# A hybrid decoder step: token sums on one engine, a denser threshold search, and value projections tied to the gathered scores

## Chip, core and metric

The kernel runs on one core of a Trainium2 chip. A core has TensorE (PE, matrix products into PSUM), VectorE (DVE), ScalarE (ACT), GpSimd (POOL) and SyncE (SP, which issues transfers); they share the on-chip memory SBUF and work from queues of their own, in order. The metric is the device time of one execution in microseconds; lower is better.

## The reference, cut to what matters

The step handles 1024 prompt tokens and 8 x 4 new tokens (`T = 1024`, `NS = 32`, together `TT = 1056` columns) of width 1024. After a conditioned norm, `h`, everything starts from one projection:

```python
u = h @ w_in       # split into qa, ka, va, za, qi, ki, wi, qr, kr, vr, zr, ga, gr
y_a = sparse_attention(qa, ka, va, top-256 keys by index_scores(qi, wi, ki)) * silu(za)
y_r = group_norm(retention(rotary(qr), rotary(kr), vr)) * g_ret * silu(zr)
merged = sigmoid(ga) * (y_a @ w_pa) + sigmoid(gr) * (y_r @ w_pr)
x = x + gate * (merged @ w_out);  y = rms_norm(x, g_final)
```

The prompt attends to its own keys; each new token also attends to 1024 cached keys and values that are gathered page by page. Retention runs over 8 heads, two at a time. Outputs are the tokens, the new key and value rows and the retention states, all in fp32.

## The kernel before

All large products are made in three terms from split operands: `wh`/`wl` for weights, `HH`/`HL` for tokens (a rounded high part and the rest), lines 216 to 220. A plain block of 128 output columns ("a projection") is made by `project_parts` in three chunks of 352 tokens, 24 matmuls each. Its weights are loaded as `ws`, rounded by ScalarE (L204), and the rest is taken by VectorE or GpSimd (L205); `order` lists which block's weights come next.

Instructions are traced in program order and then put into each engine's queue by a planner that works with estimated times and prefers what was traced first. `tc.issue_after(x)` keeps the instructions that it encloses behind x on x's engine. Pools of tiles have a fixed number of buffers (`bufs`); a tile whose place belonged to another waits until that one is read for the last time.

The stages, in order of time on the profiled execution:

1. Norm, index keys and queries, index scores `SC` of the prompt's blocks and `SCS` of the new tokens (to about 140 us).
2. *Sums of tokens* (`sums_of_tokens`, `last_sums`, L747 to L776). `paired_gates` makes pairs of 128-column blocks by a scheme with seven half-size products in place of eight. It needs sums and differences of the token blocks: `whole_of` joins a high and a low part (GpSimd), VectorE adds and subtracts (L756, L758, L760, L772, L774), ScalarE rounds (L740, L775), VectorE or GpSimd takes the rest (L741, L776). Meanwhile TensorE makes gate blocks 2 and 3, which ScalarE passes through tanh (L729).
3. *Paired blocks* (`paired_gates`): gate blocks 4 to 11 in four pairs, product tiles `sl`, weight forms on GpSimd (L797 to L816). Results are added by VectorE, passed through tanh and written to memory (`TG`).
4. *Retention* (`retention`, `pair`): for each of four head pairs the blocks KR, QR, VR, ZR, the chunked recurrence, and the norm, whose last instruction is `normed[p]` (L686). The attention's query block QA and key block KA of the same index fill TensorE's waits (`split_rows`, `key_rows`). Rotations use one buffer `rot` of 1056 KB; `key_rows` uses half of the same buffer for the key tile x.
5. *Search for the 256th largest score* (`pick_all`): 31 steps, one bit each. In a step VectorE counts five blocks (L1035), ScalarE counts two by signs (L1041), and small VectorE instructions set the next threshold. The steps are tied to `marks`, one for each finished chunk or product of stages 2 to 4. Behind the last step the sample rows are marked (`exact(1)`, `finish(6)`); `mark_rest` marks the prompt's six blocks (`exact(0)`, `finish(5)` to `finish(0)`, L1063 to L1089) into the masks `BI`.
6. *Gathered keys* (`past_scores`): for eight groups of four sequences' half pages, GpSimd gathers cached keys (L1221), TensorE turns them (L1252), ScalarE and VectorE copy them (L1254), TensorE scores them (L1230). The value blocks VA are projected after `past_scores(1)` in program order (L1307 to L1310); their tiles lie in the memory of the scores.
7. Gathered values, gates 12 to 15 and ZA (to about 870 us), the prompt's attention with the output of retention, and the output product.

`token_rows` turns a block into token rows for the outputs: TensorE transposes, ScalarE copies into a tile `tk` (L695), SyncE writes it out (L697).

## Time and profile before

| | |
|---|---|
| median of 3 runs | 1167.2 us (1165.26 to 1172.75) |
| profiled execution | 1164.71 us, span of the instructions 1162.9 us |
| mean granted TensorE clock | 0.981 |
| busy share of the span | PE 94%, PEld 85%, DVE 62%, ACT 42%, POOL 30% |
| the chain that ended last | PE 72%, DVE 13%, DMA 8%, ACT 3%, issue 3% |
| read / written in device memory | 141.49 / 43.33 MB |

Times in the profile are microseconds from the start of the span. A wait row reads "who waited <- what ended the wait: total, times, longest". A row of a group reads "line engine operation out<-in shapes xcount | busy us, mean ns | idle before us <-releaser". A timeline row is "start, duration, engine, line, operation", with the idle time ahead of it in brackets and what ended it. PEld is TensorE's loading of weights, which lies beside the products.

### The profile page before, as it was taken

To read this page: it belongs to the slowest core of one execution; us is meant where nothing else is said; L and a number is where in the kernel's file an instruction comes from. 1 tells how busy PE (TensorE), PEld (TensorE's weight loads), DVE (VectorE), ACT (ScalarE), POOL (GpSimd) and SP (SyncE) were. 2 spreads that over 40 slices of the span, in tenths; PEclk is the share of its full clock that TensorE was granted. 3 is DMA by queue.
4 is the path that set the end of the run, shared out by engine and by line. 5 is a ranking of instruction groups with operands and counts; after the bars stand their busy time and mean duration, and the time that the engine had idled before them with its cause. 6 is when DMAs were issued, how large, how long until landed. Compare 5 with 4: busy or idle time off the path is not lost.

```text
span 1162.9 us, 20931 instructions
## 1 busy us (share of the span) xinstructions
PE 1091.4 (94%) x8234; PEld 987.2 (85%) x8234; DVE 724.6 (62%) x1683; ACT 487.3 (42%) x945; POOL 352.2 (30%) x272
## 2 busy tenths in 40 slices
PE   6989988999999999999897898999999999999997
PEld 5767787999999999999797885777998888799776
DVE  6766399998467464865997124310327777587675
ACT  6565444664444444444231242211315666443111
POOL 0021378755524534222211234243103333200000
PEclk9989998999999999999998899999999999999999
DMA  9946212437237247247132889487666540258331
GB/s 310 292 111 177 74 49 72 132 129 219 55 125 222 56 140 204 58 133 218 50 112 83 261 250 313 146 300 272 227 242 215 217 173 21 90 179 286 121 143 55
DMA packets 159480, 189.98 MB, mean 163 GB/s; under 512 B 19013, under 2 KB 127245, under 8 KB 158294
## 3 DMA queue, kind: packets, MB, share of 16 engines
q1 hardware_dynamic: 149232, 152.35, 42.0%
q0 software_dynamic: 9856, 35.66, 9.0%
q8 instruction: 65, 1.06, 0.4%
q10 hardware_dynamic: 294, 0.63, 0.1%
q14 instruction: 33, 0.27, 0.1%
HBM read 141.49 MB, written 43.33 MB: 159 GB/s over the span
## 4 chain that ended last, share of the span: by engine, by line
PE 72%; DVE 13%; DMA 8%; ACT 3%; issue 3%; POOL 1%; SPq 0%; DVEq 0%; ACTq 0%; POOLq 0%
PE pj L218 10%; PE pj L220 10%; PE pj L219 10%; PE sl L838 6%; PE po L1411 3%; PE pj L1187 3%; PE pj L1188 3%; PE pj L1189 3%; PE pj L1570 3%; PE pj L1571 3%; PE pj L1572 3%; PE tr L1394 2%; DMA out<-tk 2%; PE str L1252 2%; DMA kv<-in_cache_v,idx 2%
## 5 line engine op out<-in xcount | busy, mean ns | idle before, releaser
L218 PE MATMUL pj<-hh,wh 128*128 128x352 f32 (+1 forms) x976 | 322.8, 331 | 12.8 <-ACT rot L481 6.6
L220 PE MATMUL pj<-hh,wl 128*128 128x352 f32 (+1 forms) x976 | 320.2, 328 | 0.0
L219 PE MATMUL pj<-hl,wh 128*128 128x352 f32 (+1 forms) x976 | 318.6, 326 | 0.0
L218 PEld LDWEIGHTS pj<-hh,wh 128*128 128x128 f32 x976 | 186.0, 191 | 22.8 <-issue 8.1
L220 PEld LDWEIGHTS pj<-hh,wl 128*128 128x128 f32 x976 | 186.1, 191 | 5.3 <-issue 4.2
L219 PEld LDWEIGHTS pj<-hl,wh 128*128 128x128 f32 x976 | 186.2, 191 | 1.1 <-issue 0.8
L1035 DVE TENSOR_SCALAR_CACHE_REDUCE bi<-sc,cand 128x896 bf16<-128x896 f32 (+4 forms) x155 | 135.6, 875 | 2.8
L205 POOL TENSOR_TENSOR wl<-ws,wh 128x1024 fp32r<-128x1024 f32 x31 | 76.4, 2463 | 198.6 <-ACT wh L204 193.7
L204 ACT CAST wh<-ws 128x1024 fp32r<-128x1024 f32 (+1 forms) x57 | 52.7, 928 | 86.4 <-PE pj L219 50.4
L1381 POOL TENSOR_SCALAR lg<-lg,st 128x1024 f32<-128x1024 f32 (+7 forms) x64 | 47.8, 755 | 120.1 <-DVE st L1380 107.8
L205 DVE TENSOR_TENSOR wl<-ws,wh 128x512 fp32r<-128x512 f32 (+1 forms) x26 | 25.6, 987 | 57.9 <-ACT wh L204 57.7
L1379 ACT ACTIVATE lg<-lg,st 128x1024 f32<-128x1024 f32 (+7 forms) x64 | 49.5, 774 | 25.0 <-DVE st L1378 23.3
L1570 PE MATMUL pj<-woh,MH 128*128 128x512 f32 (+1 forms) x136 | 51.4, 378 | 0.0
L1571 PE MATMUL pj<-wol,MH 128*128 128x512 f32 (+1 forms) x136 | 51.2, 377 | 0.0
L1572 PE MATMUL pj<-woh,ML 128*128 128x512 f32 (+1 forms) x136 | 51.2, 376 | 0.0
L1221 POOL DMA_INDIRECT kv<-in_cache_k,idx x32 | 30.7, 960 | 54.5 <-PE str L1252 47.3
L1221 POOL DMA_INDIRECT kv<-in_cache_v,idx x32 | 30.1, 941 | 55.0 <-PE sx L1282 43.9
L1394 PE MATMUL tr<-C,lg 128*128 128x128 f32 x288 | 43.6, 276 | 1.6 <-POOL lg L1381 0.5
L1041 ACT ACTIVATE bi<-sc,cand 128x1024 bf16<-128x1024 f32 x31 | 35.6, 1149 | 18.2 <-DVE cand L1116 18.1
L1254 DVE COPY kt<-str 128x512 f32<-128x512 f32 x32 | 22.1, 691 | 32.7 <-PE str L1252 25.1
L1252 PE MATMUL str<-C,kv 128*128 128x128 f32 x256 | 35.3, 279 | 6.8 <-DVE kt L1254 6.8
L1394 PEld LDWEIGHTS tr<-C,lg 128*128 128x128 f32 x288 | 33.3, 140 | 9.5 <-issue 2.4
(395 smaller groups left out, 2366.5 us busy)
## 6 DMA issues: line engine op xcount, KB each, us to landing
ws<-in_w_in SPq DMA_DIRECT2D x51, 512.0 KB
rot<-in_rot SPq DMA_DIRECT2D x8, 1056.0 KB
x<-in_w_ada SPq DMA_DIRECT2D x16, 512.0 KB
wst<-in_w_out SPq DMA_DIRECT2D x12, 512.0 KB
TG<-raw SPq DMA_DIRECT2D x16, 264.0 KB
u<-TG SPq DMA_DIRECT2D x8, 528.0 KB
t<-TG SPq DMA_DIRECT2D x8, 528.0 KB
x<-in_x_prompt SPq DMA_DIRECT2D x8, 512.0 KB
```

Source lines behind the costliest of these rows:

```text
L205: (nc.vector if k == 4 or not third[0] and len(order) % 3 else nc.gpsimd).tensor_sub(wl[:, :, :n], ws[:, :, :n], f32(wh[:, :, :n]))
L218: nc.tensor.matmul(p, wh[:, k], HH[k][:, sl], start=(k == 0), stop=False)
L219: nc.tensor.matmul(p, wh[:, k], HL[k][:, sl], start=False, stop=False)
L220: nc.tensor.matmul(p, wl[:, k], HH[k][:, sl], start=False, stop=(k == KT - 1))
L838: nc.tensor.matmul(x[:, 512 * g:512 * g + HB // 2], wk, mv[:, c:c + HB // 2], start=(k == 0 and term == 0), stop=(k == 3 and term == 2))
L1035: nc.vector.tensor_scalar(junk[:n, :W], sc, thr[:n, j:j + 1], 0.0, op0=op, op1=OP.add, accum_out=cnt[:n, j:j + 1])
L1221: nc.gpsimd.indirect_dma_start(out=t.rearrange("p s c -> p (s c)"), out_offset=None, in_=cache.rearrange("g (r s) h d -> (g r) (s h d)", s ...
L1252: nc.tensor.transpose(x[:, n * i + 128 * s_:n * i + 128 * s_ + 128], kst[:, s_, 128 * (p + i):128 * (p + i) + 128], ident)
L1394: nc.tensor.transpose(x[:, 128 * (j - j0):128 * (j - j0) + 128], lg[:, j % 2, 128 * (j // 2):128 * (j // 2) + 128], ident)
L1570: nc.tensor.matmul(x, MH[:, k, tk], wh[:, k], start=(k == 0), stop=False)
L1571: nc.tensor.matmul(x, MH[:, k, tk], wl[:, k], start=False, stop=False)
L1572: nc.tensor.matmul(x, ML[:, k, tk], wh[:, k], start=False, stop=(k == KT - 1))
```

## The change

- **Sums of tokens**: `whole_of` and the two GpSimd instructions of `last_sums` go to VectorE.
- **Paired blocks**: the fourth pair is no longer gates 10 and 11 but query blocks QA 0 and 1. Their results are split (ScalarE copy, VectorE sub) and written to the query rows instead of going through tanh. Gates 10 and 11 are made whole later: gate 10 behind the last head pair, gate 11 behind the value blocks.
- **Search**: marks start behind gates 2 and 3, there are 97 of them, and the steps are tied to every third mark eight times and then to every two and a half. `mark_rest` is tied behind the last pair's norm.
- **Key blocks**: `key_rows` is a generator with tiles of its own (`raw`); the low part goes chunk by chunk through the tile `zt` to memory. In head pairs 0 and 1 it fills TensorE's waits instead of QA. For the last block the token rows are copied to separate places of the rotation's buffer (`room`) instead of the one-buffer tile `tk`.
- **Value blocks**: blocks 1, 2 and 3 and gate 11 are tied behind the second, fourth, sixth and seventh score product of the gathered keys.

```diff
-    paired = [(j, j + 1) for j in range(4, 12, 2)]
+    paired = [(O_GA + 128 * j, O_GA + 128 * j + 128) for j in range(4, 10, 2)] + [(O_QA, O_QA + 128)]
     after_pairs = []
     for p in range(4):
-        after_pairs += [o + 128 * p for o in (O_KR, O_QR, O_VR, O_ZR, O_QA, O_KA)]
-    after_pairs += [O_VA + 128 * p for p in range(4)]
+        after_pairs += [o + 128 * p for o in (O_KR, O_QR, O_VR, O_ZR) + (O_QA, O_KA)[p < 2:]]
+    after_pairs += [O_GA + 1280] + [O_VA + 128 * p for p in range(4)] + [O_GA + 1408]
...
             for p in range(4):
-                rows = split_rows(gp, O_QA + 128 * p, p, q_rows, qs)
+                keys = key_rows(gp, rp, p, 1)
+                rows = split_rows(gp, O_QA + 128 * p, p, q_rows, qs) if p > 1 else keys
                 pair(rp, RC, O, SD, p, rows)
-                for _ in rows:
-                    pass
-                key_rows(gp, rp, p, rp.tile([128, 2 * TT], F32, name="rot", bufs=1)[:, :TT], 1)
+                for r in (rows, keys):
+                    for _ in r:
+                        pass
+            gates(gp, (10,))
...
-    def token_rows(tl, x, p, out_p, out_s, dst, bufs=2):
+    def token_rows(tl, x, p, out_p, out_s, dst, bufs=2, room=None):
...
-            tk = tl.tile([128, 4, 128], F32, name="tk", bufs=bufs)
+            if room is None:
+                tk = tl.tile([128, 4, 128], F32, name="tk", bufs=bufs)
+            else:
+                tk = room[:, 128 * t0:128 * t0 + 512].rearrange("p (t c) -> p t c", c=128)
...
-    def key_rows(pool, tl, p, x, bufs=2):
-        for _ in split_rows(pool, O_KA + 128 * p, p, k_rows, ks, x):
-            pass
-        token_rows(tl, x, p, k_out, ks_out, None, bufs)
+    def key_rows(pool, tl, p, bufs=2):
+        h, x = [pool.tile([128, TT], d, name="raw", bufs=rows_kept[0]) for d in (F32R, F32)]
+        rows = slice(128 * p, 128 * p + 128)
+
+        def use(c, y):
+            sl = slice(c * CH, c * CH + CH)
+            m = min(sl.stop, T) - sl.start
+            low = tl.tile([128, CH], F32, name="zt", bufs=2).bitcast(F32R)
+            nc.scalar.copy(h[:, sl], y)
+            nc.vector.tensor_sub(low, y, f32(h[:, sl]))
+            nc.scalar.copy(x[:, sl], y)
+            nc.sync.dma_start(KD[rows, 1, sl.start:sl.start + m], f32(low[:, :m]))
+            if c == 2:
+                nc.scalar.copy(ks[:, p], y[:, CH - NS:])
+        yield from project_parts(O_KA + 128 * p, use)
+        nc.sync.dma_start(KD[rows, 0], f32(h[:, :T]))
+        room = tl.tile([128, 2 * TT], F32, name="rot", bufs=1) if p == 3 else None
+        token_rows(tl, x, p, k_out, ks_out, None, bufs, room)
...
     def whole_of(x, t):
-        nc.gpsimd.tensor_tensor(t, f32(x[0]), f32(x[1]), op=OP.add)
+        nc.vector.tensor_tensor(t, f32(x[0]), f32(x[1]), op=OP.add)
...
-            nc.gpsimd.tensor_tensor(b, f32(x_), f32(y_), op=OP.subtract)
+            nc.vector.tensor_tensor(b, f32(x_), f32(y_), op=OP.subtract)
             nc.vector.tensor_tensor(a, a, b, op=OP.add)
             nc.scalar.copy(h, a)
-            nc.gpsimd.tensor_sub(l, a, f32(h))
+            nc.vector.tensor_sub(l, a, f32(h))
...
-                nc.scalar.activation(t, t, AF.Tanh, scale=0.5)
-                j = paired[n][r]
-                nc.sync.dma_start(TG[128 * j:128 * j + 128, HB * c:HB * c + HB], t)
+                f0 = paired[n][r]
+                if f0 >= O_GA:
+                    nc.scalar.activation(t, t, AF.Tanh, scale=0.5)
+                    nc.sync.dma_start(TG[f0 - O_GA:f0 - O_GA + 128, HB * c:HB * c + HB], t)
+                else:
+                    h = temp().bitcast(F32R)
+                    m_ = HB if c == 0 else T - HB
+                    nc.scalar.copy(h, t)
+                    nc.vector.tensor_sub(t.bitcast(F32R), t, f32(h))
+                    if c == 1:
+                        nc.vector.tensor_tensor(qs[:, f0 // 128], f32(h[:, m_:]), t[:, m_:], op=OP.add)
+                    for places, x in zip(q_rows, (f32(h), t)):
+                        for d in places:
+                            nc.sync.dma_start(d[f0:f0 + 128, HB * c:HB * c + m_], x[:, :m_])
...
-                after = marks[3 * i + 4 if i < 10 else 34 + 3 * (i - 10)]
+                after = marks[3 * i + 2 if i < 8 else 28 + (5 * (i - 8)) // 2]
...
         def mark_rest():
-            exact(0)
-            for j in range(NP - 2, -1, -1):
-                finish(j)
+            with tc.issue_after(normed[3].ins):
+                exact(0)
+                for j in range(NP - 2, -1, -1):
+                    finish(j)
...
-        marks = []
         with ExitStack() as s2:
...
             ps = ps1.enter_context(tc.tile_pool(name="pss", bufs=1, reuse_waits="tile", space=PSUM))
+            marks = []
             paired_gates(gp, stp, moved, lambda: ps.tile([128, 1024], F32, name="sl", bufs=4))
...
-    for p in range(4):
+    def value_rows(p):
         x = tl.tile([128, TT], F32, name="raw", bufs=rows_kept[0])
         project(O_VA + 128 * p, lambda c, y: nc.scalar.copy(x[:, c * CH:c * CH + CH], y))
         token_rows(tl, x, p, v_out, vs_out, VD)
+
+    value_rows(0)
+    for p, n in ((1, 1), (2, 3), (3, 5)):
+        with tc.issue_after(scored_[n].ins):
+            value_rows(p)
+    with tc.issue_after(scored_[6].ins):
+        gates(tl, (11,))
```

`scored_` collects the last matmul of each call of `scores` in `past_scores`.

More of the change, by code (lines that the diff above doesn't have):

```diff
@@ L459, in _hybrid_step @@
     q_rows = [[d[:, o] for o in (0, 1)] for d in QD]
-    k_rows = [[KD[:, o]] for o in (0, 1)]
     ZD = dram.tile([512, TT], F32, name="ZD")
@@ L470, in _hybrid_step, with split_rows @@
     rows_kept = [2]
-    def split_rows(pool, f0, p, dst, new, x=None):
+    def split_rows(pool, f0, p, dst, new):
         hl = [pool.tile([128, TT], F32R, name="raw", bufs=rows_kept[0]) for _ in "hl"]
@@ L479, in use @@
             nc.vector.tensor_sub(hl[1][:, sl], y, f32(hl[0][:, sl]))
-            if x is not None:
-                nc.scalar.copy(x[:, sl], y)
             if c == 2:
@@ L786, in load @@
                 t = (pool if n % 2 else wp).tile([128, KT, 128], F32, name="ws", bufs=2)
-                nc.sync.dma_start(t, wcols(w_in, KT, O_GA + 128 * paired[n][i], 128))
+                nc.sync.dma_start(t, wcols(w_in, KT, paired[n][i], 128))
                 w += [t[:, :4], t[:, 4:]]
@@ L841, in paired_gates @@
             y = inner(x)
+            temp = lambda: pool.tile([128, HB], F32, name="u", bufs=4)
             def kept(u, base):
@@ L849, in result @@
                 nc.vector.tensor_tensor(halves_(t), halves_(base), y, op=OP.add)
-                nc.scalar.activation(t, t, AF.Tanh, scale=0.5)
-                j = paired[n][r]
-                nc.sync.dma_start(TG[128 * j:128 * j + 128, HB * c:HB * c + HB], t)
-            temp = lambda: pool.tile([128, HB], F32, name="u", bufs=4)
+                f0 = paired[n][r]
[12 more added lines that the diff above has]
+                            nc.sync.dma_start(d[f0:f0 + 128, HB * c:HB * c + m_], x[:, :m_])
             if m == 1:
@@ L1147, in _hybrid_step @@
         retention(gp)
-        assert len(marks) == 106, len(marks)
+        assert len(marks) == 97, len(marks)
         drain()
@@ L1238, in scores @@
         return last
+    scored_ = []
     def past_scores(G):
@@ L1255, in past_scores @@
                 KK.append(kt)
-            scores(G, lambda b4, p: KK[b4][:, p], n, slice(n * u, n * u + n),
+            last = scores(G, lambda b4, p: KK[b4][:, p], n, slice(n * u, n * u + n),
                    BM[G][:, :PAST].rearrange("p (q s) -> p s q", s=8)[:, QU * u:QU * u + QU],
-                   st[G][:, u - 1:u] if u else BIGNEG, st[G][:, u:u + 1])
+                          st[G][:, u - 1:u] if u else BIGNEG, st[G][:, u:u + 1])
+            scored_.append(last)
     valued = []
```

## The prediction

> **What bounds the kernel now.** On the page TensorE's row of tenths stands at nine nearly everywhere, so time can come only from the slices that are lower. Behind the start-up these lie in two groups, and I cut the span there at the stages (stretch, its length, busy time of PE, PEld, DVE, ACT and POOL with counts, granted clock, DMA share, GB/s):
>
> ```profile
> 143.00:200.00 57.00, 47.03 (x299) 46.32 (x298) 56.35 (x68) 23.63 (x43) 49.24 (x32) 0.88 0.20 61
> ...
> 262.00:548.00 286.00, 285.90 (x2157) 273.48 (x2156) 176.70 (x412) 130.56 (x240) 110.28 (x53) 1.00 0.48 141
> 548.00:597.00 49.00, 44.01 (x384) 40.93 (x382) 44.88 (x85) 15.68 (x31) 8.00 (x5) 0.93 0.26 66
> 597.00:660.00 63.00, 51.52 (x300) 49.95 (x299) 37.86 (x70) 13.22 (x26) 16.89 (x11) 0.90 0.52 168
> ...
> 692.00:740.00 48.00, 38.63 (x435) 27.03 (x428) 20.82 (x39) 13.72 (x24) 23.68 (x26) 1.00 0.90 302
> ```
>
> In the sums (143 to 200) VectorE is full and TensorE idles 10.0 us; in 262 to 548 TensorE is the bound; in the last retention pair (548 to 660) it idles 5.0 and 11.5 us; over the gathered keys (692 to 740) 9.4 us. The list of waits says who ended these:
>
> ```profile
> PE str L1252 <- DVE kt L1254: 6.8, 18, 0.4
> PE pj L218 <- ACT rot L481: 6.6, 1, 6.6
> PE sl L838 <- ACT u L857: 5.6, 1, 5.6
> PE pb L601 <- DVE tmp L607: 5.0, 1, 5.0
> ...
> PE pj L218 <- ACT raw L1309: 4.1, 1, 4.1
> ...
> PE pj L218 <- ACT raw L729: 2.1, 1, 2.1
> ```
>
> ScalarE ends most of them, but it is itself held; its timeline names by whom:
>
> ```profile
> 616.14 0.45 ACT L481 COPY rot<-pj 128x352 f32<-128x352 f32 x1 [7.79 <-DVE raw L479]
> ...
> 654.47 0.25 ACT L695 COPY tk<-pt 32x128 f32<-32x128 f32 x1 [8.12 <-DMA out<-tk]
> ```
>
> So at 611 the cause is VectorE's marking, and at 652 the one-buffer tile tk, whose write to memory must land before the next copy (L1309 stands behind it on ScalarE's queue). Each long wait costs twice, for the clock falls behind it:
>
> ```profile
> 156.00:164.00 8.00, 5.92 (x28) 5.89 (x28) 7.89 (x6) 3.66 (x7) 7.41 (x5) 0.79 0.16 68
> ```
>
> This stretch holds the 2.1 us wait alone; 0.21 of 8 us is 1.7 us lost. Summed so, the clock takes 57 x 0.12 = 6.8 us in the sums and 49 x 0.07 + 63 x 0.10 = 9.7 us in the last pair. Part of it falls on idle time; I take 5.7 and 8.2, the latter as 2.9, 2.7 and 2.6 behind the three waits of that pair. The Trainium skill (TensorE: Matmul & The Clock Gate, "What's actually happening") has the rate halve after an idle window of about 3.4 us: by it a 2.1 us wait would cost no clock, and the sums would have 1.7 us less to give. The stretch above disagrees, and the sum goes by the stretch.
>
> **The change part by part.** Removable in all: sums 10.0 + 5.7 = 15.7 us, last pair 16.5 + 8.2 = 24.7 us, gathered keys 9.4 us.
>
> *Sums on VectorE.*
>
> ```profile
> 142.95 0.14 DVE L1054 TENSOR_SCALAR base<-cnt 32x1 int32<-32x1 f32 x1 [5.10 <-ACT bis L1041]
> ...
> 146.85 0.70 DVE L741 TENSOR_TENSOR tl<-u,th 128x528 fp32r<-128x528 f32 x1
> ...
> 148.83 1.83 DVE L756 TENSOR_TENSOR u<-u 128x528 f32<-128x528 f32 x1
> ...
> 167.46 0.40 PE L838 MATMUL sl<-hh,wh 128*128 128x264 f32 x2
> ...
> 188.98 72.72 PE sl L838 x576
> ...
> L744 POOL TENSOR_TENSOR u<-hh,hl 128x528 f32<-128x528 f32 x8 | 12.2, 1540 | 0.7 <-DVE tl L741 0.7
> L773 POOL TENSOR_TENSOR u<-hl,tl 128x528 f32<-128x528 f32 x4 | 6.6, 1660 | 2.0 <-DVE tl L741 2.0
> L744 POOL TENSOR_TENSOR ws<-hh,hl 128x528 f32<-128x528 f32 x4 | 6.0, 1491 | 2.7 <-DVE u L758 2.7
> L776 POOL TENSOR_TENSOR hl<-u,hh 128x528 fp32r<-128x528 f32 x4 | 5.8, 1439 | 0.0
> ```
>
> A VectorE sum of 128x528 takes 0.70 us alone and 1.83 us beside a GpSimd sum. Twenty GpSimd instructions (30.6 us) become twenty of VectorE: 14 us. With the 32 that it has, 52 x 0.70 = 36.4 us; about eight weight forms that stay on GpSimd may hold it some 1.1 us each, 9 us. VectorE waits idle until 142.95 and can begin near 138, so it ends at about 183; the first 36 instructions end near 168. The first products start at 167.46 after a 2.1 us wait and its 1.7 us of clock, so at 163.7 without them. Three need no sum (24 matmuls and 72.72 x 24 / 576 = 3.0 us each), which gives 172.7; the fourth finds its sums, the sixth (178.7) may wait for the last ones. The first search step also leaves this stage, since marks begin behind it. I keep 3 us: **-12.7**. Bounds: -15.7, and 0 if the forms hold every sum.
>
> *Query pair, gate 10 and 11 exchanged.* The four pairs keep their products; two query blocks take the place of gates 10 and 11, which are made whole later: TensorE's work is the same. Their four results swap a tanh for one copy and one VectorE sub each, 4 x 0.70 us, against six subs saved later; sixteen DMAs leave instead of four, in place of eight later. Between 262 and 548 nothing of it ends a wait: 0. Pairs 0 and 1 have two chunks of filler less, which the next pair's projections replace.
>
> *Denser search.*
>
> ```profile
> L1035 DVE TENSOR_SCALAR_CACHE_REDUCE bi<-sc,cand 128x896 bf16<-128x896 f32 (+4 forms) x155 | 135.6, 875 | 2.8
> ...
> 624.89 0.45 ACT L1309 COPY raw<-pj 128x352 f32<-128x352 f32 x1 [3.36 <-PE pj L220]
> 628.71 0.45 ACT L1309 COPY raw<-pj 128x352 f32<-128x352 f32 x1 [3.36 <-PE pj L220]
> ```
>
> 155 counts are 31 steps of five: 4.4 us of counts, with their small instructions about 5.3 us. A chunk of a projection takes 3.8 us, so a step per 2.5 chunks is one per 9.6 us instead of 11.5. 262 to 548 gets two steps more in 23 us less: (176.7 + 10.6) / 263 = 71% of VectorE, under TensorE's cover. The last step falls on the second chunk of the last pair's values, one chunk later in that pair than now, so the marking of the sample rows, which follows at once, still meets the products behind L607. I halve that wait (5.0 + 2.9 of clock): **-4.0**, bounds -7.9 and 0.
>
> *Marking behind the last norm; tk in the rotation's tile.* At L481 VectorE has nothing to mark any more: **-9.3** (6.6 + 2.7). With a place of its own for each group, ScalarE's copies of the last key tile no longer wait for memory: **-6.7** (4.1 + 2.6). Key tiles in raw free the rotation's buffer for the next pair's load; no TensorE wait stands there: 0.
>
> What is late next? The marking itself (groups of VectorE between 578 and 632; then the norm's place in the first and the last pair, idx, the first gather and the gathers' median landing):
>
> ```profile
> L1086 DVE TENSOR_TENSOR_SCAN ra<-eq 128x1024 f32<-128x1024 bf16 (+5 forms) x6 | 9.7, 1623 | 0.1
> L1088 DVE SCALAR_TENSOR_TENSOR ra<-sc,base,ra 128x1024 f32<-128x1024 f32 (+5 forms) x6 | 7.4, 1237 | 0.0
> L1087 DVE SCALAR_TENSOR_TENSOR ra<-ra,rem,eq 128x1024 f32<-128x1024 f32 (+5 forms) x6 | 7.4, 1230 | 0.1
> L1035 DVE TENSOR_SCALAR_CACHE_REDUCE eq<-sc,base 128x1024 bf16<-128x1024 f32 (+5 forms) x7 | 6.9, 987 | 0.0
> L1085 DVE TENSOR_SCALAR eq<-sc,base 128x1024 bf16<-128x1024 f32 (+5 forms) x6 | 3.4, 574 | 0.0
> L1089 DVE TENSOR_SCALAR bi<-ra 128x1024 bf16<-128x1024 f32 (+5 forms) x6 | 3.1, 518 | 0.0
> ...
> 626.29 0.39 DVE L1211 TENSOR_SCALAR idx<-gidx 128x8 int32<-128x8 int32 x4 [0.98 <-DMA kd<-raw]
> ...
> L655 PE MATMUL pt<-vm,kd x16: 587/613/638, 328.1 to 596.6; 32*64 32x512 f32 x16
> ...
> L683 PE MATMUL pt<-C,O x36: 243/272/327, 345.2 to 638.6; 128*128 128x128 f32 x32, 32*128 32x32 f32 x4
> ...
> 639.58 1.04 POOL L1221 DMA_INDIRECT kv<-in_cache_k,idx  x1 [3.26 <-issue]
> ...
> kv<-in_cache_k,idx POOLq DMA_INDIRECT x32, 6.4
> ```
>
> The six groups sum to 38 us. In the first pair the norm's transposes (L683) begin 17 us behind L655; in the last one, in the marking's company, they end 42 us behind it. So without company the last norm ends near 618 instead of 639, and the marking, which now waits for it, runs from there to 656 or later. The value tiles lie where the scores were: the first over the three smallest blocks, which are marked after the largest, so it is free after some two thirds, near 643; the last only at the end. Until then TensorE has from 597 on 6.75 chunks of queries, keys and gate 10 (26 us), two value chunks into its two banks (7.6 us) and 2.5 us of transposes: to 633. The first gather needs idx (it waited for a key tile's write, KD from raw, above), whose place gate 10's raw tile may now hold until its own write lands near 628; 6.4 us later it is there. So TensorE stands still for 2 to 10 us; I take 5 and 2.5 of clock: **+7.5**. Behind the marking on VectorE's queue come the copies of the gathered keys (L1254), for which the transposes wait: at worst a scan of 1.6 us for each of the first eight gathers, 13 us, at best nothing; I take **+5**.
>
> *Values held.* Three value blocks and gate 11 now stand between the scores instead of ahead of them, and fill TensorE's short waits for L1254. The holds bind TensorE's queue alone. The weight splits of these blocks move along, onto GpSimd's queue among the gathers or VectorE's behind the marking; seven buffers of gathers cover them, without which one such split delays a gather by its length. SyncE gets eight more issues for the keys' low parts and the value writes later; nothing on the path waits for it there, but the value rows of the new tokens must land before the second phase, beside gate 11 as cover. The first two of eight steps stay bare, so I take two thirds of 9.4: **-6.3**; bounds -9.4 and 0.
>
> Sum: -12.7 - 4.0 - 9.3 - 6.7 + 7.5 + 5 - 6.3 = -26.5. The profiled execution took 1164.71 us (span 1162.9), 2.5 us under the median of 1167.2; between 1138.2 and 1140.7 I say **1139 us**.
>
> **The rivals.** *All waits go and none comes*: 15.7 + 24.7 + 9.4 = 49.8 us off, 1117. For it: none of the fills is short on paper; against: the 38 us of marking have to stand somewhere.
>
> *The marking takes the place of what it held before.* If the first value tile too waits for all of it (23 us from 633 to 656) and the copies pay their 13 us, then 36 us stand against the 34.1 that the last pair and the gathered keys have to give (24.7 + 9.4): the sums alone remain, 1167.2 - 12.7 = 1154.5. For it: the memory that both share; against: fillers and gathers are there before 643.
>
> *Gathers starved.*
>
> ```profile
> 670.64 1.57 POOL L1221 DMA_INDIRECT kv<-in_cache_k,idx  x1 [3.12 <-PE str L1252]
> ```
>
> One gather's issue took 1.57 us, beside a VectorE sub, against 0.94 otherwise. With the marking beside the gathers, the steps L1085 and L1089 (6.5 us) could hold the first ones up: 1139 + 6.5 = 1145. The Trainium skill (SBUF — State Buffer, "Who interferes with whom") says so of such instructions: the port pair is an exclusive lock, and GpSimd writes its descriptors through it.
>
> *Slower: the keys' low parts.* They now go through tile zt, two buffers, each to land in memory before its next use.
>
> ```profile
> 443.58 4.97 DMA out<-tk
> ...
> 646.02 8.35 DMA out<-tk
> ```
>
> Two chunks cover 7.6 us. A landing of 5.0 us is hidden; 8.4 costs 0.8 a chunk. From about 11 us on, twelve chunks would stall 3.4 us each, VectorE's queue with the search behind them: +41, 1180. For it: the freed rotation buffer lets 1056 KB loads run at the same time. Against: both rows are shorter, and the longer one stood among gathers.
>
> *It doesn't do it*: each engine's order is fixed beforehand from estimated times; if it comes out with the same blockages, 1165.
>
> **How the numbers follow.** Forecast 0.50 (1127 to 1150), all gone 0.12, marking in the way 0.18, starved 0.07, same blockages 0.06, slower 0.07. The range 1117 to 1160 leaves out the slower case, the unchanged one and a tail below. 1% (11.7 us) is about what a measurement here tells from no change; the marking case straddles that line, two thirds on the faster side: faster 0.81, same 0.12, slower 0.07.
>
> **What would show it.** Right: no TensorE wait over 3 us between 143 and 200, granted clock above 0.95 there, L741 and L756 near 0.7 us; no wait on L481 or for tk; L1086 to L1089 after the last L686; projections between the L1252 groups. Wrong: a wait for the value tiles' copies or for gathers above 10 us; waits for zt; VectorE full in 262 to 548 with TensorE idle.

## The result, and the profile after

The changed kernel took 1150.8 us in the median of four runs (1147.99 to 1153.95), the kernel before 1166.58 us beside it: a ratio of 0.9858, 95% interval 0.982 to 0.9896. It is faster, by 15.8 us where 28 were forecast. The profiled execution took 1151.78 us (span 1150.0, against 1162.9). The spans differ by 12.9 us only, and four variants below that add next to nothing (experiments 2, 3, 7 and 8) have ratios of 0.989 to 0.991, so some 13 us is the better estimate of what the change is worth.

I cut both spans at the same four events: the end of the index scores, the end of the paired products (end of A), the end of the last head pair's state products (end of B, the retention) and the end of the gathered keys' scores (end of C). Columns as in the prediction: stretch, length, busy time of PE, PEld, DVE, ACT and POOL with counts, granted clock, DMA share, GB/s. First the windows of the kernel before, then of the changed one:

```profile
140.40:261.69 121.29, 111.32 (x817) 110.61 (x818) 116.73 (x206) 66.44 (x116) 90.39 (x63) 0.94 0.29 92
261.69:597.18 335.49, 330.40 (x2542) 314.79 (x2540) 222.05 (x498) 146.24 (x270) 118.35 (x58) 0.99 0.45 130
597.18:739.28 142.10, 121.02 (x969) 105.54 (x969) 65.08 (x117) 39.55 (x75) 49.87 (x44) 0.95 0.71 229
```

```profile
141.76:256.49 114.73, 106.92 (x817) 106.71 (x818) 104.41 (x198) 60.86 (x107) 79.13 (x45) 0.97 0.31 100
256.49:572.12 315.63, 305.02 (x2389) 291.53 (x2387) 228.09 (x496) 144.02 (x269) 113.83 (x56) 0.98 0.45 130
572.12:727.49 155.37, 142.88 (x1122) 127.28 (x1122) 78.49 (x144) 45.04 (x84) 53.45 (x45) 0.97 0.68 219
```

B lost 153 products and C gained 153; at 3.8 us for a chunk of 24 these are 24.2 us of work that only moved. Without them A changed by -6.6, B by +4.3 (315.63 + 24.2 - 335.49) and C by -10.9 us (155.37 - 24.2 - 142.10). What comes before and behind adds +1.4 and -1.1; together -12.9, the difference of the spans. The sums, then, gave half of what was forecast, and the retention got no shorter. How much longer it got is less sure than +4.3: variants below with the same code there scatter from 309.7 to 317.2 us in B, against 311.3 (335.49 - 24.2) in the one trace of before.

The list of waits of the changed kernel, the largest behind the start-up (who waited <- what ended it: total, times, longest):

```profile
PE pb L600 <- DVE tmp L606: 9.6, 4, 3.8
PE sl L854 <- POOL wh L832: 7.8, 1, 7.8
PE str L1283 <- DMA kv<-in_cache_k,idx: 5.1, 2, 3.2
PE str L1283 <- ACT kt L1285: 4.6, 8, 0.7
```

L600 (L601 before) waited once before (5.0 us, last pair) and now waits in all four pairs. Gone are the waits for the rotation's copy (6.6) and behind the tile tk (4.1), and of the key transposes' wait for copies (6.8 on VectorE) 5.1 is left. New are a weight form of GpSimd and the gathers. The timelines of GpSimd and VectorE name what stood behind these two (start, duration, engine, line):

```profile
153.99 19.10 POOL L832 TENSOR_TENSOR wh<-ws,wh 128x512 fp32r<-128x512 f32 x1 [6.79 <-ACT wh L831]
173.05 1.27 POOL L832 TENSOR_TENSOR wl<-ws,wl 128x512 fp32r<-128x512 f32 x1
...
307.43 2.33 POOL L205 TENSOR_TENSOR wl<-ws,wh 128x1024 fp32r<-128x1024 f32 x1
...
608.23 1.19 POOL L1250 DMA_INDIRECT kv<-in_cache_k,idx  x1 [16.76 <-DVE idx L1240]
```

```profile
154.56 0.70 DVE L757 TENSOR_TENSOR tl<-u,th 128x528 fp32r<-128x528 f32 x1
...
171.27 0.70 DVE L790 TENSOR_TENSOR u<-u 128x528 f32<-128x528 f32 x1
...
306.40 0.61 DVE L1063 TENSOR_SCALAR_CACHE_REDUCE bi<-sc,cand 128x384 bf16<-128x384 f32 x1
...
306.94 3.21 DVE L576 SCALAR_TENSOR_TENSOR zsT<-zt,zsT 128x352 f32<-128x352 f32 x1
...
382.91 3.42 DVE L576 SCALAR_TENSOR_TENSOR zsT<-zt,zsT 128x352 f32<-128x352 f32 x1
...
457.12 0.51 DVE L576 SCALAR_TENSOR_TENSOR zsT<-zt,zsT 128x352 f32<-128x352 f32 x1
...
462.04 1.95 DVE L576 SCALAR_TENSOR_TENSOR zsT<-zt,zsT 128x352 f32<-128x352 f32 x1
...
592.67 0.25 DVE L685 SCALAR_TENSOR_TENSOR tmp<-pt,gT,zsT 128x32 f32<-128x32 f32 x1 [2.29 <-PE pt L682]
592.84 0.14 DVE L1091 TENSOR_SCALAR low<-base 128x1 f32<-128x1 f32 x1
...
607.20 0.38 DVE L1240 TENSOR_SCALAR idx<-gidx 128x8 int32<-128x8 int32 x4
```

VectorE's sums now follow one another at 0.70 us without a pause, 28 of them from 154.56 to 171.97, and one GpSimd sub that takes 1.27 us behind them takes 19.1 beside them. The marking begins right behind the last norm, as the tie says, but the gather indices (L1240) stand 14 us into it on VectorE's queue, so the first gather starts at 608. VectorE's mask products (L606) free the PSUM tiles for which L600 waits. The zsT instruction (the pair's gate) right ahead of them takes 3.2, 3.4 and 1.95 us in pairs 0 to 2, where the shortest (an earlier chunk of pair 2) takes 0.51, and the last of a search step's five counts (L1063) stands right ahead of it. Pair 0 before the change, with ScalarE's copy from which zsT goes on, and that copy after the change:

```profile
310.16 0.44 ACT L576 COPY zsT<-pj 128x352 f32<-128x352 f32 x1
...
310.64 2.08 DVE L577 SCALAR_TENSOR_TENSOR zsT<-zt,zsT 128x352 f32<-128x352 f32 x1 [3.53 <-ACT zsT L576]
```

```profile
304.99 0.44 ACT L575 COPY zsT<-pj 128x352 f32<-128x352 f32 x1
```

### The profile page after: what moved, and what is told of

It reads as the page before. It is cut to its first block, busy times and chain, and to the rows that moved or that the text cites. A ratio compares the mean times of both kernels' runs of the same rounds, so it can differ in the third digit from the quotient of the medians.

```text
span 1150.0 us, 20968 instructions
## 1 busy us (share of the span) xinstructions
PE 1085.6 (94%) x8233; PEld 982.7 (85%) x8234; DVE 734.3 (64%) x1704; ACT 484.9 (42%) x943; POOL 336.7 (29%) x251
## 4 chain that ended last, share of the span: by engine, by line
PE 75%; DVE 10%; DMA 6%; issue 4%; POOL 3%; ACT 2%; SPq 1%; DVEq 0%; ACTq 0%; POOLq 0%
PE pj L218 11%; PE pj L220 10%; PE pj L219 10%; PE sl L854 7%; PE po L1450 3%; PE pj L1216 3%; PE pj L1218 3%; PE pj L1217 3%; PE pj L1609 3%; PE pj L1610 3%; PE pj L1611 3%; PE tr L1433 2%; PE str L1283 2%; DVE bi L1063 2%; POOL wh L832 2%
## 5 line engine op out<-in xcount | busy, mean ns | idle before, releaser
L1063 DVE TENSOR_SCALAR_CACHE_REDUCE bi<-sc,cand 128x896 bf16<-128x896 f32 (+4 forms) x155 | 135.9, 877 | 2.6
L205 POOL TENSOR_TENSOR wl<-ws,wh 128x1024 fp32r<-128x1024 f32 x30 | 73.3, 2444 | 194.9 <-ACT wh L204 179.4
L1250 POOL DMA_INDIRECT kv<-in_cache_k,idx x32 | 34.7, 1083 | 63.7 <-PE str L1283 43.1
L1283 PE MATMUL str<-C,kv 128*128 128x128 f32 x256 | 38.3, 291 | 11.9 <-DMA kv<-in_cache_k,idx 5.1
L1285 ACT COPY kt<-str 128x512 f32<-128x512 f32 x32 | 18.8, 586 | 72.9 <-PE str L1283 63.6
L1283 PEld LDWEIGHTS str<-C,kv 128*128 128x128 f32 x256 | 30.3, 147 | 19.6 <-issue 7.6
```

The lines of the kernel that those rows point to most:

```text
L205: (nc.vector if k == 4 or not third[0] and len(order) % 3 else nc.gpsimd).tensor_sub(wl[:, :, :n], ws[:, :, :n], f32(wh[:, :, :n]))
L1063: nc.vector.tensor_scalar(junk[:n, :W], sc, thr[:n, j:j + 1], 0.0, op0=op, op1=OP.add, accum_out=cnt[:n, j:j + 1])
L1250: nc.gpsimd.indirect_dma_start(out=t.rearrange("p s c -> p (s c)"), out_offset=None, in_=cache.rearrange("g (r s) h d -> (g r) (s h d)", s ...
L1283: nc.tensor.transpose(x[:, n * i + 128 * s_:n * i + 128 * s_ + 128], kst[:, s_, 128 * (p + i):128 * (p + i) + 128], ident)
```

## The experiments

The kernel before had medians of 1163.5 to 1164.3 us in these runs against 1166.6 beside the result, so times are compared as ratios. Where two variants lie within half a percent, I read the lengths of the stages in their profiled runs. B varied between 309.7 and 317.2 us among the variants that leave its search and its products alone (experiments 1 to 3, 6 to 9 and 11). Nearly all of that scatter is in the first three head pairs (217.8 to 225.1 us); the last pair took 91.3 to 92.8 us in all variants but two. So in B only a length outside these ranges, or a wait that is gone, is taken as an effect.

**1. Sums back on GpSimd.**

```diff
-        nc.vector.tensor_tensor(t, f32(x[0]), f32(x[1]), op=OP.add)
+        nc.gpsimd.tensor_tensor(t, f32(x[0]), f32(x[1]), op=OP.add)
...
-            nc.vector.tensor_tensor(b, f32(x_), f32(y_), op=OP.subtract)
+            nc.gpsimd.tensor_tensor(b, f32(x_), f32(y_), op=OP.subtract)
...
-            nc.vector.tensor_sub(l, a, f32(h))
+            nc.gpsimd.tensor_sub(l, a, f32(h))
```

> The changed kernel with the sums of the token blocks back on GpSimd as before the change (the joining of high and low parts, and two of the five instructions of the last sums). Theory A: the move to VectorE is worth what the two traces show up to the end of the paired blocks, about 5 us of the 15.8 us that the whole change brought: 1156 us, the three short waits of before (2.1, 2.3, 5.6 us) return and the 7.8 us wait for the weight form goes. Theory B: it is worth the 12.7 us of the prediction: 1163.5. Theory C: the move only exchanges one wait for another: 1151, within 2 us of the changed kernel.

Measured: 1156.77 us, ratio 0.9943 (0.9919 to 0.9967). The window of stage A:

```profile
140.28:260.96 120.68, 110.97 (x818) 110.26 (x819) 109.81 (x179) 60.10 (x106) 89.86 (x63) 0.94 0.29 93
```

120.68 against 114.73: the move is worth 6.0 us in its stage, and the clock goes from 0.97 back to 0.94. Theory A. By the ratios the difference is 0.85%, or 10 us, with an uncertainty that would not exclude 12.7; but the other stages of the two profiles differ by under 2 us, and against the 0.989 to 0.991 of experiments 2, 3, 7 and 8 it is 4 to 6 us.

**2. The first weight forms on VectorE.**

```diff
-            nc.gpsimd.tensor_sub(w[:, 4:], x, f32(w[:, :4]))
+            (nc.vector if i < 3 else nc.gpsimd).tensor_sub(w[:, 4:], x, f32(w[:, :4]))
```

> The changed kernel with the low parts of the first three weight forms on VectorE instead of GpSimd (three subs of 128x512). Theory A: GpSimd's one sub of 19.1 us is held up by VectorE's unbroken row of sums, and only the wait for it keeps TensorE idle for 7.8 us and then at half rate for about 7 us (3.4 us lost): these go for some 2 us of VectorE's time, so 7 to 10 us less than the changed kernel, about 1142. Theory B: the products would then wait for the sums themselves, which end at 171: within 2 us of 1150.8, with a wait of sl on a VectorE or ScalarE row of the sums in its place.

Measured: 1152.16 us, ratio 0.9909 (0.988 to 0.9937); A 114.58 us. The wait of 7.8 us is gone and another has come, by the list of waits and ScalarE's timeline:

```profile
PE sl L854 <- ACT u L885: 5.8, 1, 5.8
```

```profile
184.46 0.63 ACT L791 CAST hh<-u 128x528 fp32r<-128x528 f32 x1 [4.08 <-DVE u L790]
185.00 0.59 ACT L885 COPY u<-sl 128x528 f32<-128x528 f32 x1
```

The fifth product needs the PSUM tile of the first, whose copy (L885) stands behind a rounding (L791) that waits for VectorE's sums. Theory B: one wait takes the place of the other.

**3. Last sums traced later**, behind the second product inside `paired_gates` instead of ahead of it; beside the edit of experiment 2:

```diff
-            last_sums(stp, moved)
...
-                p1 = temp()
+                p1 = out[1][:, :HB] if n == 0 else temp()
...
+            if i == 1:
+                last_sums(pool, moved)
```

> The variant with the first three weight forms on VectorE, and besides with the last sums traced behind the second product instead of ahead of the first, so that ScalarE's copy of the first product stands ahead of the last sums' four roundings in its queue (its copy goes to a half of the second result's tile). Theory A: with the forms on VectorE TensorE stood for 5.85 us ahead of the fifth product only because the first product's copy on ScalarE stood behind roundings that wait for VectorE; that wait and its half rate (3.4 us) shrink: from the end of the index scores to the end of the paired products 106 to 109 us instead of 114.6, in all about 1145. Theory B: VectorE's 52 sums and three forms at 0.70 us set the end of this stage, in whatever order: the wait moves to the sixth product, which needs the last sums, and the stage stays within 2 us of 114.6.

Measured: 1150.29 us, ratio 0.9889 (0.9848 to 0.9931). Window of stage A and its waits:

```profile
139.92:252.81 112.89, 108.39 (x818) 107.76 (x818) 106.90 (x202) 61.48 (x107) 63.14 (x42) 0.97 0.32 104
```

```profile
PE sl L854 <- DVE hl L792: 2.9, 2, 1.9
PE sl L854 <- ACT hh L791: 1.6, 1, 1.6
```

1.8 us less than the changed kernel: Theory B. TensorE waits for the last sums themselves, in the sixth product. In seven of the other variants, whose sums are those of the changed kernel, the wait for GpSimd's form was only 2.5 us long, the last sums ended another of 2.4, and A still was 113.1 to 114.5 us. VectorE's sums set the length of this stage, as far as these runs show, whichever wait shows it.

**4. Search steps moved by a chunk.**

```diff
-                after = marks[3 * i + 2 if i < 8 else 28 + (5 * (i - 8)) // 2]
+            steps = [3 * i + 2 for i in range(8)] + [b + j for b in (28, 43, 58) for j in (0, 2, 4, 7, 9, 12)] + [73, 75, 78, 80, 83]
+                after = marks[steps[i]]
```

> The changed kernel with the same number of search steps, but in head pairs 0 to 2 each step that was tied to the second chunk of ZR is tied to the first one, and in pairs 0 to 2 two others move one chunk. Theory A: the waits of TensorE for the masked scores (2.6, 2.0 and 1.2 us in pairs 0 to 2, and 1.7 us at half rate) come from a step's counts that stand right ahead of the mask products on VectorE, behind which the last zsT instruction then falls together with GpSimd's weight split (3.2 and 3.4 us where it takes 0.5 alone): they go, 5 to 7 us less than the changed kernel, about 1145. Theory B: it is the number of steps in the stage, not their place: the waits stay or move, within 2 us of 1150.8.

Measured: 1162.95 us, ratio 0.9986 (0.9961 to 1.0012): about 1% slower than the changed kernel, which neither theory said. Its ten times lie in two groups, three from 1154.7 to 1157.8 us and seven from 1162.6 to 1165.9; the profile (1162.63) is of the longer one. The windows of stage B and of a piece of it, and ScalarE's timeline ahead of that piece:

```profile
255.24:583.22 327.98, 313.99 (x2388) 298.56 (x2387) 230.10 (x496) 144.46 (x269) 113.71 (x56) 0.96 0.43 126
467.00:478.00 11.00, 11.00 (x93) 9.84 (x87) 6.95 (x13) 3.67 (x7) 2.35 (x1) 0.50 0.20 53
```

```profile
463.28 1.15 ACT L1069 ACTIVATE bi<-sc,cand 128x1024 bf16<-128x1024 f32 x1 [5.81 <-DVE cand L1145]
...
465.58 0.56 ACT L566 COPY kd<-pt 128x512 f32<-128x512 f32 x1
```

B is 12.4 us longer with the same products. TensorE waited 2.6 us for the norm's instructions and once 4.1 us for a copy of the keys (L566, pair 2), and ran at half rate behind that. The timeline says what held the copy: the step's counts by signs (L1069) stand ahead of it on ScalarE's queue, and they wait 5.8 us for the next threshold (`cand`), which VectorE makes behind its own counts. So a step can block TensorE by ScalarE's queue too. Where a step falls matters by more than I had thought; the other places that moved weren't traced.

**5. A shorter search.**

```diff
-            for k in range(30, -1, -1):
+            for k in range(30, 6, -1):
...
-                after = marks[3 * i + 2 if i < 8 else 28 + (5 * (i - 8)) // 2]
+                after = marks[3 * i + 2 if i < 8 else 28 + (11 * (i - 8)) // 3]
```

> The changed kernel with 24 search steps instead of 31 (the threshold's last seven bits are left out), eight in the paired blocks as in the changed kernel and 16 instead of 23 in the retention, ending at the same place of the last head pair. Theory A: the load of the counts on VectorE makes the new waits of TensorE for the masked scores in pairs 0 to 2 (5.8 us and 1.7 us of clock): they go, and the stretch from the end of the paired products to the end of the last pair's state products shrinks from 315.6 to about 308 us; the wait of 3.8 us in the last pair stays, since the marking of the sample rows stands where it stood. Theory B: the waits come from what fills the pairs (key blocks in place of query blocks) or from GpSimd's weight splits alone: the stretch stays within 2 us of 315.6, and zsT instructions of 3 us stay.

Measured: 1154.65 us, ratio 0.9912 (0.9886 to 0.9939). Window of B, and the zsT instruction of pair 1 on VectorE's timeline:

```profile
254.13:569.71 315.58, 308.13 (x2389) 293.24 (x2387) 175.26 (x392) 129.04 (x241) 114.17 (x56) 0.98 0.44 130
```

```profile
379.04 3.12 DVE L576 SCALAR_TENSOR_TENSOR zsT<-zt,zsT 128x352 f32<-128x352 f32 x1
```

VectorE has 53 us less to do in B, and B is as long. The waits of L600 in pairs 0 and 2 went or nearly so, that of pair 1 stayed (1.0 us) with a zsT instruction of 3.1 us, one other came (1.3) and the wait for the key copy (L566) grew from 1.0 to 1.2. The load of the counts alone is not the cause; Theory A falls and Theory B holds. The edit moves the steps' places as well as their number, though: in pair 0 no counts stand ahead of zsT any more, and there the wait is gone.

**6. Marking not tied to the norm.**

```diff
-            with tc.issue_after(normed[3].ins):
-                exact(0)
-                for j in range(NP - 2, -1, -1):
-                    finish(j)
+            exact(0)
+            for j in range(NP - 2, -1, -1):
+                finish(j)
```

> The changed kernel without the tie of the marking of the prompt's blocks to the last pair's norm, which is where the kernel before had it. Theory A: the tie removed the wait for the rotation's copy in the last pair (6.6 us and 2.7 of clock): it comes back, and the stretch from the last state products to the end of the gathered keys' scores grows from 155.4 us by 6 to 10. Theory B: the marking, begun some 15 us earlier, is out of the way of the gathered keys' copies and of the gather indices, and what is lost ahead of the norm is won there: within 3 us of the changed kernel, with shorter waits among the gathered keys. Theory C: the whole is faster by 3 us or more, so that the tie costs time.

Measured: 1162.46 us, ratio 0.9987 (0.9968 to 1.0007); C 167.26 us, 11.9 more. Its waits and ScalarE's timeline:

```profile
PE str L1282 <- ACT kt L1284: 17.2, 3, 16.7
...
PE pj L218 <- ACT ks L719: 2.3, 1, 2.3
```

```profile
593.49 0.45 ACT L716 COPY raw<-pj 128x352 f32<-128x352 f32 x1 [5.53 <-DVE zt L715]
...
634.18 0.26 ACT L697 COPY tk<-pt 32x128 f32<-32x128 f32 x1 [17.76 <-DMA VD<-tk]
```

The size is Theory A's, the place only in part. A small piece of the wait that the tie was to remove is back: ScalarE's copy of the last key block (L716) is held 5.5 us by VectorE's sub (L715), which stands in the marking, and TensorE waits 2.3 us for the copy behind it. The larger piece is another: with the marking early, the first value block's memory is free early, its token rows are copied among the first gathers, and the last of these copies waits 17.8 us for the tile's write, ahead of the key copies on ScalarE.

**7. One tile tk.**

```diff
-        room = tl.tile([128, 2 * TT], F32, name="rot", bufs=1) if p == 3 else None
+        room = None
```

> The changed kernel with the last key block's token rows copied through the one-buffer tile again instead of to places of their own in the rotation's buffer. Theory A: the wait of before comes back (8.1 us on ScalarE for the tile's write, 4.1 us on TensorE and 2.6 of clock), now ahead of gate 10 or the first value block: 4 to 7 us more than the changed kernel. Theory B: gate 10 and the held value blocks give TensorE enough else to do: within 2 us, with ScalarE waiting but TensorE not.

Measured: 1151.58 us, ratio 0.9895 (0.9854 to 0.9937). ScalarE's timeline and the window from 569 to the end of C:

```profile
594.42 0.59 ACT L697 COPY tk<-pt 128x512 f32<-128x512 f32 x1 [3.02 <-DMA out<-tk]
...
598.99 0.26 ACT L697 COPY tk<-pt 32x128 f32<-32x128 f32 x1 [3.61 <-DMA out<-tk]
```

```profile
569.00:724.32 155.32, 142.24 (x1121) 127.01 (x1122) 78.17 (x144) 44.92 (x84) 55.56 (x45) 0.98 0.69 219
```

Theory B: ScalarE waits, TensorE has other work, C is 155.3 and 155.4 us.

**8. Value blocks not tied.**

```diff
-    for p, n in ((1, 1), (2, 3), (3, 5)):
-        with tc.issue_after(scored_[n].ins):
-            value_rows(p)
+    for p in (1, 2, 3):
+        value_rows(p)
...
-    with tc.issue_after(scored_[6].ins):
-        gates(tl, (11,))
+    gates(tl, (11,))
```

> The changed kernel with value blocks 1 to 3 and gate 11 no longer tied behind the score products of the gathered keys: they stand where program order and the planner put them. Theory A (the prediction's term of 6.3 us): TensorE does them ahead of the gathered keys' last groups and then waits for copies and gathers between bare groups; the stretch from the last state products to the end of the gathered keys' scores stays about 155 us or grows by 4 to 8, and small waits return behind it. Theory B: what the tie holds back is ScalarE's copy of value rows whose tile waits for a write among the gathers; without it such a copy stands ahead of key copies, and one wait of over 10 us appears: 10 us or more. Theory C: nothing, within 3 us of 1150.8.

Measured: 1153.31 us, ratio 0.9908 (0.9881 to 0.9934); C 155.14 against 155.37 us. Theory C: the tie is worth nothing here.

**9. Gather indices early.**

```diff
             nc.vector.tensor_tensor(gidx, ptab, gio, op=OP.add)
+            idx = selp.tile([128, 4, NB], I32, name="idx")
+            for u in range(4):
+                nc.vector.tensor_scalar(idx[:, u], gidx, 4.0, float(u), op0=OP.mult, op1=OP.add)
...
-    idx = sv.tile([128, NQ, NB], I32, name="idx")
-    for u in range(NQ):
-        nc.vector.tensor_scalar(idx[:, u], gidx, float(NQ), float(u), op0=OP.mult, op1=OP.add)
```

> The changed kernel with the gather indices made once, right behind the page addresses in the first stage, instead of behind the retention, where VectorE reaches them at 607.2 after 14 us of marking. Theory A: the first gathers are late because of that place on VectorE's queue: they start near 592 instead of 608, the waits for gathered keys (3.2 and 1.9 us) and the half rate behind them (about 4 us) shrink, 4 to 8 us less, about 1145. Theory B: the gathers then wait for their buffers or for the transfer's traffic, or TensorE waits on VectorE's copies of the gathered keys between the marking: within 2 us of 1150.8.

Measured: 1142.92 us, ratio 0.9842 (0.9807 to 0.9878). GpSimd's timeline and the window of C:

```profile
589.47 0.99 POOL L1250 DMA_INDIRECT kv<-in_cache_k,idx  x1 [1.96 <-PE pj L220]
```

```profile
568.15:717.72 149.57, 141.02 (x1123) 126.01 (x1122) 77.66 (x140) 44.83 (x84) 53.64 (x45) 0.99 0.72 227
```

The first gather starts 19 us earlier, the wait for gathers (5.1 us) is gone, C is 5.8 us shorter: Theory A. The ratio alone doesn't tell it from the changed kernel's.

**10. Sample rows' marking later**, with the early indices:

```diff
-            exact(1)
-            finish(NP - 1)
+            with tc.issue_after(marks[88][0]):
+                exact(1)
+                finish(NP - 1)
```

> The variant with the gather indices made early, and besides with the marking of the sample rows (some 11 us of VectorE) tied behind the first chunk of the last pair's query block instead of following the last search step. Theory A: the sample rows' marking is what the last pair's mask products wait behind (3.8 us and 3.4 us at half rate): both go, 5 to 7 us less than the variant with the early indices alone (1142.9). Theory B: the marking then falls between the last norm's small instructions, the norm ends later, and the tied marking of the prompt's blocks, the first value tile and the gathered keys' copies behind it: within 3 us of 1142.9, or slower.

Measured: 1142.25 us, ratio 0.9815 (0.9788 to 0.9842). Windows of B and C, and of the last pair alone (from the end of pair 2's state products), here and in the changed kernel:

```profile
255.29:561.53 306.24, 300.76 (x2388) 287.74 (x2386) 219.82 (x493) 144.49 (x269) 112.56 (x56) 1.00 0.45 133
561.53:712.49 150.96, 140.51 (x1123) 126.85 (x1123) 79.09 (x143) 45.52 (x84) 53.04 (x45) 0.99 0.73 229
...
475.58:561.53 85.95, 85.56 (x665) 82.40 (x665) 61.38 (x135) 37.31 (x70) 21.58 (x11) 1.00 0.40 119
```

```profile
480.18:572.12 91.94, 88.13 (x666) 84.54 (x666) 66.61 (x138) 37.16 (x70) 22.76 (x11) 0.96 0.40 118
```

The last pair's wait fell from 3.8 to 0.4 us, the half rate behind it went, and B is 6.2 us shorter than with the indices alone; C gives 1.4 back. The last pair takes 85.95 us, in experiment 12 too, where all other variants have 91.3 to 92.8. Theory A in the profile, which is the shortest of this variant's four runs; between the two ratios the gain (0.3%) doesn't show.

**11. Gate 11 behind gate 10**, with the early indices:

```diff
...
-            gates(gp, (10,))
+            gates(gp, (10, 11))
...
-    with tc.issue_after(scored_[6].ins):
-        gates(tl, (11,))
```

> The variant with the gather indices made early, and besides with gate 11 projected right behind gate 10, in the tiles of the retention's stage, instead of behind the seventh score product. Theory A: the first gathered groups stand bare between copies because the value tiles' memory is taken by the marking until about 643; gate 11 needs none of it and fills 11.5 us there: the waits of 0.4 to 0.9 us among the first groups (7.7 us in all) shrink by half, 1142.9 less 3 to 5. Theory B: TensorE does the gate ahead of the first groups rather than between them, the small waits stay, and the end lacks a filler: within 2 us of 1142.9, or slower by up to 5.

Measured: 1145.84 us, ratio 0.9828 (0.9798 to 0.9858); C 153.77 us, 4.2 longer than with the indices alone. Theory B: TensorE made the gate first and then waited for VectorE's copies of the keys (5.7 us, the longest 3.8), since VectorE was still marking. That is read from the profile alone, of the longest of the four runs; the ratios of the two variants don't separate them.

**12. Copies of the first half of the gathered keys on ScalarE**, with the edits of 9 and 10:

```diff
-                    (nc.vector.tensor_copy if p else nc.scalar.copy)(kt[:, p:p + 2] ...
+                    (nc.vector.tensor_copy if p and G else nc.scalar.copy)(kt[:, p:p + 2] ...
```

> The variant with early gather indices and the later marking of the sample rows, and besides with all copies of the first half of the gathered keys on ScalarE instead of every second one on VectorE. Theory A: between 600 and 635 VectorE is full with the marking (39.6 of 40 us) and its copies of the keys stand in that queue, which is what TensorE's waits of 0.35 to 1.15 us there (9.3 us in all, with 1.7 at half rate) come from; ScalarE has 30 of 40 us free: the waits shrink by half, 3 to 6 us less than that variant (1142.3), about 1138, and the stretch from the last state products to the end of the gathered keys' scores shrinks from 151.0 to 146 or so. Theory B: with two PSUM tiles and one engine for the copies the transposes wait for ScalarE (0.59 us a copy and its latency against 0.66 us of transposes) as often as before: within 2 us of 1142.3.

Measured: **1128.3 us** (1126.64 to 1130.86), ratio 0.9694 (0.9674 to 0.9713). The windows of A, B and C, and the largest wait of TensorE in C:

```profile
140.44:253.54 113.10, 108.06 (x818) 107.57 (x818) 105.05 (x197) 60.30 (x107) 72.93 (x45) 0.98 0.32 101
253.54:561.69 308.15, 302.28 (x2387) 289.26 (x2386) 220.50 (x493) 144.24 (x269) 112.61 (x56) 0.99 0.45 132
561.69:703.96 142.27, 139.04 (x1122) 125.36 (x1123) 70.45 (x127) 52.76 (x100) 54.49 (x45) 1.00 0.76 243
```

```profile
PE str L1284 <- ACT kt L1286: 2.3, 11, 0.2
```

C falls by 8.7 us, TensorE is busy in 139.0 of its 142.3 us at full clock, and the longest wait of a transpose is 0.2 us. More than Theory A said: it was the queue behind the marking, not the two PSUM tiles. This version beats the kernel before by 3.1% and the changed one by a margin that the intervals separate.

## Why the prediction was right in sign and short in size

The sum was -26.5 and the span gave -12.9. By stage: A -12.7 forecast and -6.6 measured; B -4.0 and +4.3 (with the scatter named above); C -9.8 (-9.3 - 6.7 + 7.5 + 5 - 6.3) and -10.9.

**Sums: mis-sized.** The row of 0.70 us came true, and TensorE's first product came at 164.7 where 163.7 was worked out. What failed is "I keep 3 us": 7.8 us of idle time and some 3.4 of clock stayed (114.73 x 0.03). I counted GpSimd's forms as a load on VectorE of about 1.1 us each; instead one of them was held for 19.1 us beside VectorE's sums. But that was not the price. Experiments 2 and 3 took that wait away and got the next, down to the last sums themselves: moving twenty instructions onto the engine that is full makes them cheaper, not free. The Trainium skill (SBUF — State Buffer, "Who interferes with whom") calls the port pair that VectorE and GpSimd share an exclusive lock; GpSimd's 19.1 us beside 28 unbroken sums agrees with a lock, though no run here separates it from other causes.

**Search at no cost: wrong.** The account put the exchange of the query pair ("nothing of it ends a wait") and the denser search (71% of VectorE, "under TensorE's cover") at nothing between 262 and 548. VectorE was busy 72% of B (228.09 of 315.63), as worked out, and still TensorE waited 5.8 us at L600 in pairs 0 to 2. A share says nothing of the moment. In pairs 0 and 1 the last zsT ended 2.1 us behind ScalarE's copy before the change, and ends 4.7 and 4.3 us behind it now: it stands 1.5 and 0.9 us behind a step's counts, and it takes 1.1 and 1.4 us longer itself, with GpSimd's work beside it (a weight split runs from 307.4 to 309.8). What goes beyond 2.1 us is the wait, to within 0.1 us, in these two pairs of the changed kernel and of every variant but experiment 4's. So the place of the steps made a part of these waits and the longer zsT the rest; why more of GpSimd's work falls beside zsT now stays open, and the exchanged filler blocks were not tested alone. Experiment 5 shows that fewer steps don't shorten the stage, experiment 4 that other places can cost 12 us.

**The halved wait (-4.0).** It fell from 5.0 to 3.8 us and kept its half rate. The last pair took 95.1 us before and takes 91.9 now; nine products that moved to other pairs are 1.4 us of that, so 1.7 us were won of the 4.0. The argument that the last step is one chunk later in the pair was too coarse; experiment 10 shows the cause, the sample rows' marking, and removes it.

**Last pair and gathered keys: right sum, wrong terms.** The tie (-9.3) does keep 12 us of C, but the wait that its absence brings is mostly another one (experiment 6): of the 6.6 us at the last key block's copy 2.3 come back without it. That the key tiles of their own removed the rest is likely, and only argued. The separate places for the token rows (-6.7) and the tied value blocks (-6.3) are worth nothing in C (experiments 7 and 8); that gate 10 and the planner's own order cover both is my reading, not tested. On the other side TensorE did not wait for the value tiles. The late first gather was real (5.1 us of waits), by idx's place behind 14 us of marking rather than by its memory: on VectorE's timeline idx follows the marking without idle time. Experiment 9 gives it another tile as well as an earlier place, so it doesn't separate the two. The copies behind the marking cost more than the +5: experiment 12 took 8.7 us out of C by them. The wait behind the tile tk (4.1 us) did go, but it goes with one tile too, so another part of the change took it. That the stage's sum came out near is luck: its terms don't hold one by one.

**The rivals.** The marking did in part take the place of what it had held, as that rival said, through the key copies. Gathers were issued a little slower beside the marking (1083 ns in the mean, 960 before), far from what the rival of starved gathers had; waits for zt and the unchanged blockages did not show. Of the marks named ahead, the order of L1091 behind the norm, the 0.70 us and the absent tk wait of TensorE came true; the 7.8 us wait in the sums broke the first, and the granted clock from 143 to 200 was 0.94, not above 0.95.

**The clock.** That a wait of about 2 us can cost a piece of half rate, as the prediction took from its own stretch, shows again. The changed kernel behind the wait of 2.6 us at L600 in pair 0, and behind that of 2.0 us in pair 1:

```profile
310.90:320.00 9.10, 9.10 (x90) 8.60 (x91) 6.67 (x16) 6.01 (x9) 0.00 (x0) 1.00 0.29 83
388.10:391.50 3.40, 3.40 (x14) 3.40 (x13) 1.94 (x3) 1.98 (x2) 0.00 (x0) 0.50 0.31 94
```

The longer wait cost nothing and the shorter one 1.7 us (half of 3.4), so its length alone doesn't tell what a wait costs. The Trainium skill (TensorE: Matmul & The Clock Gate, "What's actually happening") has the rate fall after an idle window of about 3.4 us; 3.4 us is the length of the slow piece here, not of the idle time ahead of it.

## What to carry to other kernels

A busy share of a stage tells whether an engine can become its bound, not whether an instruction is late; read what stands ahead of each instruction that TensorE waits for, on its own queue, and move the work that may wait (the marking) or the copies that may not (onto the engine with room). When a wait goes, ask at once for the next: in the sums three different waits covered the same VectorE time. And test each part of a change alone, for two parts here were worth nothing and four small instructions, 0.4 us together, in the wrong place were worth six.

## What the hardware showed that I had not expected

One GpSimd sub of 128x512 took 19.1 us beside an unbroken row of VectorE sums, and 1.27 us behind it. A VectorE instruction of 0.51 us (the shortest zsT) took up to 3.42 us, with GpSimd at work beside it. And in experiment 4 a wait of 4.1 us was followed by a long piece at half rate: the 11 us from 467 to 478 lie within it, with TensorE busy throughout.
